# Attention scores kept as negatives with a running minimum, one reciprocal per group, and the output weights' casts queued behind the last exponential

## The chip, the cores and the metric

The kernel runs on one core of one Trainium2 chip. The metric is device time in microseconds (us) of one execution. The core has a matrix engine (TensorE, PE in the profile; PEld is its weight load), a vector engine (VectorE, DVE), an activation engine (ScalarE, ACT), GpSimd (POOL) and a queue that issues DMAs (SyncE, SP). Each engine works through its own queue strictly in order.

## The reference, cut to what matters

One decoder layer: half of the heads do dilated attention, half an mLSTM; the two are concatenated, projected with `w_out`, normalised, and followed by a mixture of 32 experts and a second normalisation. The change touches the attention heads alone, and the moment at which `w_out` is prepared.

```python
scores = einsum('bhrnqe,bhrnke->bhrnqk', qs, kb) * e ** -0.5
m = max(scores, axis=-1, keepdims=True)
p = exp(scores - m)
l = sum(p, axis=-1, keepdims=True)
o = einsum('bhrnqk,bhrnke->bhrnqe', p / l, vb)
...
y = concatenate([attn, hm], axis=-1) @ w_out
```

The kernel folds the three dilated branches into one softmax with an additive mask `am`: the logarithm of how often a key is counted, or -1e30 where it isn't seen.

## The kernel before, in words

The program is written with a planner: the Python order of the code is the priority, and the planner puts each engine's instructions into one fixed queue, in which something of lower priority goes first where the planner expects the higher one to be still waiting. `tc.high_priority` raises a block's priority. `tc.issue_after(ins)` queues every instruction of a block that runs on the engine of `ins` behind `ins` in that engine's queue; instructions of the block on other engines are not bound by it, except through their data.

The mixer takes the first 490 us, roughly, of the span. Its attention part loops over four pairs of heads, j = 0 to 3. A pair has 8 tiles of 128 queries for each of its 2 heads, in two groups: `scores(o, 0)` does query tiles 0 to 3, `scores(o, 1)` tiles 4 to 7 (lines 507 to 531). For query tile i the keys are 128*(i+1) long and are handled in pieces of up to 512 columns. Per piece two matmuls write the PSUM tile `s` (three buffers), and one fused DVE instruction (line 525, in the trace a CUSTOM_DVE with a short accumulator read behind it) adds the mask, writes the sum to SBUF as `p`, and keeps the running maximum in `mx`. Then, per tile and head, DVE negates the maximum (line 528), ACT computes the exponential in place with that bias and sums the row (line 529), and DVE takes the reciprocal of the sum (line 530). That is 64 tiles, 96 pieces.

`values(j, o, g, ...)` (lines 533 to 564) transposes the weights `p` on PE, copies them to SBUF (one head on ACT, the other on DVE), multiplies with the values (line 550), transposes the result back (line 559), and one DVE multiplication (line 561, `ao`) applies the reciprocals `rl` of the whole group. A DMA then writes `ao` to `mixd`.

Between these, `mlstm(c)` does chunk c of the mLSTM heads and `qk_proj(j + 1)` projects queries and keys of the next pair. The order is: `scores(o, 1)`, `mlstm(2j)`, `values(.., 0)`, then `qk_proj(j + 1)` or, for j = 3, `out_weights()`, then `mlstm(2j + 1)`, the next pair's `scores(o2, 0)`, and `values(.., 1)`.

`out_weights()` (lines 569 to 578) loads `w_out` in 8 parts of 128 rows into two buffers `woraw`, and splits each into a high part `woh` (ACT cast, line 111) and a low part `wol` (DVE subtraction, line 112, in the helper `split`). A buffer takes its next part only when the DVE subtraction of the part two before it is done; the DMA for that waits at the head of SP's queue. After the pairs, `project(t, n)` multiplies the mixed rows with `woh` and `wol` (line 683), and the rest of the kernel follows: routing, experts, final normalisation.

Of the kernel before, what the change touches and what calls it, by code (L numbers as in the profile page):

```python
# [14 lines left out]
AF = mybir.ActivationFunctionType  # L15
OP = mybir.AluOpType
# [14 lines left out]
NEG = -1.0e30  # L31
# [74 lines left out]
class Build:  # L106
# [29 lines left out]
    def mixer(self):  # L136
        nc, tc, I, C = self.nc, self.tc, self.I, self.C
# [176 lines left out]
        for g, dst in ((0, ip), (1, fp)):  # L314
            for hf in range(2):
                pt = ps.tile([4, 512], F32, name="m", bufs=1, padded_shape=[128, 512])
                for t in range(4):
# [15 lines left out]
                                     op0=OP.max, op1=OP.add)  # L333
# [31 lines left out]
        def qk_proj(j):  # L365
            hi, lo = [], []
            for g in range(2):
                raw, h, l = chunk([128, 4, 2, 128], "qk")
                for w in range(2):
                    nc.sync.dma_start(raw[:, :, w], I["w_in"][g * 512:(g + 1) * 512,  # L370
                                                            w * 512 + j * 128:w * 512 + (j + 1) * 128].rearrange(
                        "(k p) f -> p k f", p=128))
                self.split(h, l, raw)
                hi.append(h)
                lo.append(l)
            for w, dst, scale in ((0, qd, 0.125), (1, kd, 1.0)):
                for n in range(2):
                    ns = slice(n * 512, (n + 1) * 512)

                    def evict(a_):  # L380
                        h_ = self.pq.tile([128, 512], F32R, name="qh", tag="ev", bufs=4)
                        l_ = self.pq.tile([128, 512], F32R, name="ql", tag="ev", bufs=4)
                        nc.scalar.activation(h_, a_, AF.Copy, scale=scale)
                        nc.vector.scalar_tensor_tensor(l_, a_, scale, h_.bitcast(F32), op0=OP.mult, op1=OP.subtract)
                        for h in range(2):
                            nc.sync.dma_start(dst[2 * j + h, 0, :, ns], h_[64 * h:64 * h + 64].bitcast(F32))
                            nc.sync.dma_start(dst[2 * j + h, 1, :, ns], l_[64 * h:64 * h + 64].bitcast(F32))

                    w_tile(lambda k: (hi[k // 4][:, k % 4, w], lo[k // 4][:, k % 4, w]), n, evict)
# [3 lines left out]
        am = po.tile([128, S], F32, name="am")  # L393
# [113 lines left out]
        def scores(o, g):  # L507

            P = {}
            rl = pt_.tile([128, 4, 2], F32, name="rl", bufs=3)  # L510
            for i in range(4 * g, 4 * g + 4):
                nk = (i + 1) * 128
                off = S - nk
                for h in range(2):
                    q, kh, kl = o[h]
                    p = P[h, i] = pt_.tile([128, nk], F32, name=f"p{i}", bufs=2)
                    mx = pt_.tile([128, 4], F32, name="mx", bufs=4)
                    for n, a in enumerate(range(0, nk, 512)):
                        b = min(nk, a + 512)
                        s_ = ps.tile([128, 512], F32, name="s", bufs=N_S)  # L520
                        nc.tensor.matmul(s_[:, :b - a], q[:, i * 128:(i + 1) * 128], kh[:, a:b],
                                         start=True, stop=False)
                        nc.tensor.matmul(s_[:, :b - a], q[:, i * 128:(i + 1) * 128], kl[:, a:b],
                                         start=False, stop=True)
                        nc.vector.tensor_tensor_reduce(p[:, a:b], s_[:, :b - a], am[:, off + a:off + b], 1.0,
                                                       NEG if n == 0 else mx[:, 0:1], op0=OP.add, op1=OP.max,
                                                       accum_out=mx[:, n:n + 1])
                    nc.vector.tensor_scalar(mx[:, 2:3], mx[:, n:n + 1], -1.0, None, op0=OP.mult)
                    nc.scalar.activation(p, p, AF.Exp, bias=mx[:, 2:3], accum_out=mx[:, 3:4])
                    nc.vector.reciprocal(rl[:, i - 4 * g, h:h + 1], mx[:, 3:4])  # L530
            return P, rl

        def values(j, o, g, P, rl):

            oT = ps.tile([128, 512], F32, name="pv", bufs=1)
            nk = 4 * g + 4
            for k in range(nk):
                i0 = max(k, 4 * g)
                n = nk - i0
                pT, ev = [], []  # L540
                for h in range(2):
                    tp = ps.tile([128, 4, 128], F32, name="pT", bufs=N_PT)
                    for i in range(i0, nk):
                        nc.tensor.transpose(tp[:, i - i0], P[h, i][:, k * 128:(k + 1) * 128], ident)
                    t = pt_.tile([128, 4, 128], F32, name="pTs", bufs=N_PTS)
                    ev.append((nc.vector.tensor_copy if h else nc.scalar.copy)(t[:, :n], tp[:, :n]))
                    pT.append(t)

                with tc.high_priority(PAIR):
                    mms = [nc.tensor.matmul(oT[64 * h:64 * h + 64, (4 - n) * 128:], o["v"][:, k, 64 * h:64 * h + 64],  # L550
                                            pT[h][:, :n].rearrange("p a b -> p (a b)"), start=k == 0,
                                            stop=k == nk - 1, skip_group_check=True) for h in range(2)]
                self.after(mms[0], ev[1], mybir.DependencyClass.Sync)
                self.after(mms[1], mms[0])
            os_ = pt_.tile([128, 512], F32, name="os", tag="os", bufs=1)
            nc.scalar.copy(os_, oT)
            tp = ps.tile([128, 4, 128], F32, name="pT", bufs=N_PT)
            for i in range(4):
                nc.tensor.transpose(tp[:, i], os_[:, i * 128:(i + 1) * 128], ident)
            ao = pt_.tile([128, 4, 2, 64], F32, name="ao", tag="os", bufs=1)  # L560
            nc.vector.tensor_tensor(ao, tp.rearrange("p a (h e) -> p a h e", h=2),
                                    rl[:, :, :, None].to_broadcast([128, 4, 2, 64]), op=OP.mult)
            nc.sync.dma_start(mixd[g * 512:(g + 1) * 512, j * 128:(j + 1) * 128].rearrange("(a p) e -> p a e", p=128),
                              ao.rearrange("p a h e -> p a (h e)"))
# [4 lines left out]
        def out_weights():  # L569
            nonlocal pw, px, woh, wol  # L570
            pw = tc.alloc_tile_pool(name="pw", bufs=1, side="right", reuse_waits="tile")
            woh = pw.tile([128, 8, D], F32R, name="woh")
            wol = pw.tile([128, 8, D], F32R, name="wol")
            for k in range(8):
                raw = pw.tile([128, D], F32, name="woraw", bufs=2)
                nc.sync.dma_start(raw, I["w_out"][k * 128:(k + 1) * 128, :])
                self.split(woh[:, k, :], wol[:, k, :], raw)
            px = tc.alloc_tile_pool(name="px", bufs=1, side="right", reuse_waits="tile")
# [3 lines left out]
        def mixed(t):  # L582

            mx = px.tile([128, D], F32, name="mixt", bufs=2)
            nc.sync.dma_start(mx, mixd[t * 128:(t + 1) * 128, :])
            mh = px.tile([128, 8, 128], F32R, name="mh", bufs=2)
            ml = px.tile([128, 8, 128], F32R, name="ml", bufs=2)
            for g in range(2):
                tp = ps.tile([128, 4, 128], F32, name="s", bufs=N_S)
                for j in range(4):  # L590
                    nc.tensor.transpose(tp[:, j], mx[:, (4 * g + j) * 128:(4 * g + j + 1) * 128], ident)
                self.split(mh[:, 4 * g:4 * g + 4], ml[:, 4 * g:4 * g + 4], tp)
            mT[t] = mh, ml

        P0 = scores(o, 0)
        for j in range(4):
            P1 = scores(o, 1)
            mlstm(2 * j)
            values(j, o, 0, *P0)
            if j < 3:  # L600
                qk_proj(j + 1)
            else:
                self.pq.release()
                pa.release()
                out_weights()
                with tc.high_priority(PAIR):
                    mixed(0)
                split = self.lastv
            mlstm(2 * j + 1)
            if j < 3:  # L610
                o2 = operands(j + 1)
                P0 = scores(o2, 0)
            values(j, o, 1, *P1)
            if j < 3:
                o = o2
# [935 lines left out]
```

## Time and profile before

| what | us |
|---|---|
| median of 3 runs | 2060.92 (2059.4 to 2061.57) |
| the profiled execution | 2062.43 |
| span of the profiled execution | 2060.8 |
| PE busy | 1978.8 (96%) |
| DVE busy | 1531.8 (74%) |
| ACT busy | 1214.6 (59%) |

The span is the time from the first to the last instruction that the profiler recorded; the execution's own time lies 1.63 us above it. Busy times are sums over the whole span, and stages differ much. In the rows further down, a time in us from the span's start stands first, then a duration, the engine, the line of the kernel, the operation, output and input, and in brackets how long the engine sat idle before it and what ended that. "issue" there means that the wait was for nothing that the profile can name.

### The profile page before, as it was taken

The numbers are of one execution on the slowest core, as the hardware profiler recorded it, in microseconds if no ns is written. First come the engines' busy times: TensorE is split into PE (matmuls) and PEld (weight loads), VectorE is DVE, ScalarE is ACT, GpSimd is POOL, SyncE is SP. The second block draws the span as 40 slices with busy tenths as digits, with TensorE's granted clock in tenths as the row PEclk, the third lists the DMA queues.
The fourth block names the chain that finished last, engine by engine and source line by source line (L and its number), as shares of the span: only waits on it lengthen the run. The fifth ranks groups of instructions, "written<-read, shape, count | busy, mean of one in ns | idle before, by whom it ended". The sixth has DMA issues, their size and how long they took to land.

```text
span 2060.8 us, 33562 instructions
## 1 busy us (share of the span) xinstructions
PE 1978.8 (96%) x11575; PEld 1506.2 (73%) x11575; DVE 1531.8 (74%) x2351; ACT 1214.6 (59%) x1668; POOL 336.0 (16%) x162
## 2 busy tenths in 40 slices
PE   8999999989988999999999999999999999999992
PEld 7987676756766886677777777777777777777771
DVE  4263554576878686777979889798797887987886
ACT  4232544462226565666767767677676776766774
POOL 0000100100002030322303213033131330310100
PEclk9999999999998999999999999999999999999996
DMA  7327465556329678787988989989889898898985
GB/s 245 100 79 184 114 163 151 138 171 198 142 86 367 243 257 301 263 321 279 363 301 325 350 298 337 329 317 364 288 335 339 310 367 285 338 312 297 357 343 184
DMA packets 194782, 543.18 MB, mean 264 GB/s; under 512 B 23964, under 2 KB 60100, under 8 KB 194604
## 3 DMA queue, kind: packets, MB, share of 16 engines
q1 hardware_dynamic: 179760, 493.28, 66.4%
q0 software_dynamic: 13840, 44.57, 8.6%
q10 hardware_dynamic: 1008, 3.15, 0.4%
q8 instruction: 92, 1.51, 0.3%
q14 instruction: 82, 0.67, 0.1%
HBM read 486.10 MB, written 54.82 MB: 262 GB/s over the span
## 4 chain that ended last, share of the span: by engine, by line
PE 71%; DVE 3%; DMA 2%; ACT 1%; issue 1%; SPq 0%; DVEq 0%; POOLq 0%; ACTq 0%
PE mm L1162 53%; PE fold L1171 8%; PE tr L1125 3%; PE acc L683 2%; PE mm L1178 1%; PE s L683 1%; DMA acc<-ym,idx 1%; DMA raw<-in_w_gate 0%; PE tr L1047 0%; PE pv L550 0%; PE tr L1114 0%; DMA xt<-in_x 0%; ACT fs L1486 0%; PE pv L743 0%; DMA woraw<-in_w_out 0%
## 5 line engine op out<-in xcount | busy, mean ns | idle before, releaser
L112 DVE TENSOR_TENSOR wlo<-raw,whi 128x1024 fp32r<-128x1024 f32 x768 | 914.3, 1224 | 193.9 <-ACT whi L111 171.1
L111 ACT CAST whi<-raw 128x1024 fp32r<-128x1024 f32 x768 | 804.8, 1052 | 313.2 <-PE mm L1162 271.4
L1162 PE MATMUL mm<-whi,xh 128*128 128x512 f32 x1040 | 336.0, 404 | 0.0
L1162 PE MATMUL mm<-wlo,xh 128*128 128x512 f32 x1040 | 323.2, 392 | 0.0
L1162 PE MATMUL mm<-whi,xl 128*128 128x512 f32 x1040 | 321.8, 391 | 0.0
L1097 POOL DMA_INDIRECT acc<-ym,idx x35 | 69.6, 1988 | 985.1 <-DVE lst L1078 494.3
L1162 PEld LDWEIGHTS mm<-whi,xh 128*128 128x128 f32 x1040 | 186.2, 188 | 59.8 <-issue 24.0
L1162 PEld LDWEIGHTS mm<-whi,xl 128*128 128x128 f32 x1040 | 195.5, 188 | 43.0
L1162 PEld LDWEIGHTS mm<-wlo,xh 128*128 128x128 f32 x1040 | 195.6, 188 | 42.7
L1162 PE MATMUL mm<-whi,hh 128*128 128x512 f32 x528 | 169.6, 402 | 0.7 <-ACT hh L111 0.7
L1162 PE MATMUL mm<-whi,hl 128*128 128x512 f32 x528 | 166.2, 395 | 0.0
L1162 PE MATMUL mm<-wlo,hh 128*128 128x512 f32 x528 | 166.1, 395 | 0.0
L1092 POOL DMA_INDIRECT xm<-hs,idx x35 | 111.5, 3187 | 54.1 <-PE mm L1162 26.9
L1162 PEld LDWEIGHTS mm<-wlo,hh 128*128 128x128 f32 x528 | 99.4, 188 | 23.3
L1162 PEld LDWEIGHTS mm<-whi,hl 128*128 128x128 f32 x528 | 99.2, 188 | 23.2
L1162 PEld LDWEIGHTS mm<-whi,hh 128*128 128x128 f32 x528 | 96.1, 188 | 25.7 <-issue 4.9
L1092 POOL DMA_INDIRECT xf<-hs,idx x12 | 101.4, 8452 | 3.7 <-issue 3.7
L1171 PE MATMUL fold<-raw,xf 128*32 128x256 f32 x1536 | 87.9, 381 | 0.0
L238 PE MATMUL acc<-xh,whi 128*128 128x512 f32 x192 | 78.1, 407 | 0.1
L238 PE MATMUL acc<-xh,wlo 128*128 128x512 f32 x192 | 77.1, 402 | 0.0
L238 PE MATMUL acc<-xl,whi 128*128 128x512 f32 x192 | 76.8, 400 | 0.0
L1171 PEld LDWEIGHTS fold<-raw,xf 128*32 128x32 f32 x1536 | 47.3, 110 | 33.7 <-issue 4.7
(385 smaller groups left out, 2766.1 us busy)
## 6 DMA issues: line engine op xcount, KB each, us to landing
raw<-in_w_down SPq DMA_DIRECT2D x256, 512.0 KB
raw<-in_w_gate SPq DMA_DIRECT2D x252, 512.0 KB
raw<-in_w_up SPq DMA_DIRECT2D x252, 512.0 KB
wraw<-in_w_in SPq DMA_DIRECT2D x24, 256.0 KB
wraw<-in_w_in SPq DMA_DIRECT2D x8, 512.0 KB
aq<-qd SPq DMA_DIRECT2D x8, 512.0 KB
akh<-kd SPq DMA_DIRECT2D x16, 256.0 KB
akl<-kd SPq DMA_DIRECT2D x16, 256.0 KB
```

Of the source, the lines that this page charges most:

```text
L111: self.lasts = self.nc.scalar.copy(hi, src)
L112: self.lastv = self.nc.vector.tensor_tensor(lo, src, hi.bitcast(F32), op=OP.subtract)
L238: nc.tensor.matmul(a_, w, x[:, k, ns], start=(k == 0 and i == 0), stop=(k == 7 and i == 2))
L683: self.projected = nc.tensor.matmul(a_, a[:, k], b[:, k, ns], start=(k == 0 and i == 0), stop=(k == 7 and i == 2))
L1092: self.gathered = self.nc.gpsimd.indirect_dma_start(xg, None, self.rows(self.hs, kind), bass.IndirectOffsetOnAxis(ap=idx[:, u:u + 1], axis=0))
L1097: self.nc.gpsimd.indirect_dma_start(self.rows(self.acc, kind), bass.IndirectOffsetOnAxis(ap=idx[:, u:u + 1], axis=0), y, None, compute_op= ...
L1125: self.turned = nc.tensor.transpose(tp[:, j], x[:, (4 * g + j) * 128:(4 * g + j + 1) * 128], ident)
L1162: self.multiplied = nc.tensor.matmul(outs[n], a[:, kk], b[k][:, n * 512:(n + 1) * 512], start=first and kk == 0 and i == 0, stop=kk == 7 a ...
L1171: nc.tensor.matmul(out[m * g:m * g + m], x[:, kk % n, (kk // n) * m:(kk // n) * m + m], raw[:, g * w:(g + 1) * w], start=first and kk == 0 ...
L1178: self.nc.tensor.matmul(outs[n], self.ones[32 * n:32 * n + 3], brow[32 * n:32 * n + 3, w], start=first, stop=False)
```

## The change

Scores are written with the opposite sign: the fused DVE instruction now scales the masked sum by -1 and keeps a running minimum, which starts at +1e30. The minimum of the negatives is minus the maximum, so it serves as the bias of the exponential as it is, and the exponential takes a scale of -1. The sum of a row is written by ACT straight into its column of the group's tile `rl`, and `values` inverts that tile (128 x 8 values) with one reciprocal, in place, ahead of the multiplication. The block `out_weights()` is traced inside `issue_after` of the last exponential that has been traced, which for j = 3 is that of tile 7, head 1.

```diff
-    nc.vector.tensor_tensor_reduce(p[:, a:b], s_[:, :b - a], am[:, off + a:off + b], 1.0,
-                                   NEG if n == 0 else mx[:, 0:1], op0=OP.add, op1=OP.max,
+    nc.vector.tensor_tensor_reduce(p[:, a:b], s_[:, :b - a], am[:, off + a:off + b], -1.0,
+                                   -NEG if n == 0 else mx[:, 0:1], op0=OP.add, op1=OP.min,
                                    accum_out=mx[:, n:n + 1])
-nc.vector.tensor_scalar(mx[:, 2:3], mx[:, n:n + 1], -1.0, None, op0=OP.mult)
-nc.scalar.activation(p, p, AF.Exp, bias=mx[:, 2:3], accum_out=mx[:, 3:4])
-nc.vector.reciprocal(rl[:, i - 4 * g, h:h + 1], mx[:, 3:4])
+self.weighed = nc.scalar.activation(p, p, AF.Exp, bias=mx[:, n:n + 1], scale=-1.0,
+                                    accum_out=rl[:, i - 4 * g, h:h + 1])
...
+            nc.vector.reciprocal(rl, rl)
             nc.vector.tensor_tensor(ao, tp.rearrange("p a (h e) -> p a h e", h=2),
                                     rl[:, :, :, None].to_broadcast([128, 4, 2, 64]), op=OP.mult)
...
-                out_weights()
+                with tc.issue_after(self.weighed.ins):
+                    out_weights()
```

## Rows read from the trace of the kernel before

**Rows 1.** The page: busy time of PE, and the chain that ended last, by engine.
```profile
PE 1978.8 (96%) x11575; PEld 1506.2 (73%) x11575; DVE 1531.8 (74%) x2351; ACT 1214.6 (59%) x1668; POOL 336.0 (16%) x162
...
PE 71%; DVE 3%; DMA 2%; ACT 1%; issue 1%; SPq 0%; DVEq 0%; POOLq 0%; ACTq 0%
```

**Rows 2.** Timeline of PE where it sat idle, in the four stretches of scores.
```profile
222.55 0.33 PE L544 MATMUL pT<-cst,p 128*128 128x128 f32 x1 [0.54 <-ACT p L529]
...
233.49 0.68 PE L472 MATMUL m<-va,w 128*128 128x129 f32 x4 [2.23 <-issue]
...
310.17 0.49 PE L498 MATMUL m<-va,kw 128*128 128x129 f32 x2 [1.86 <-DVE mx L528]
...
375.06 0.46 PE L472 MATMUL m<-va,w 128*128 128x129 f32 x2 [0.65 <-DVE rl L530]
...
438.53 0.50 PE L521 MATMUL s<-akh,aq 128*128 128x512 f32 x1 [0.89 <-DVE mx L525]
443.06 0.77 PE L472 MATMUL m<-va,w 128*128 128x129 f32 x2 [2.46 <-issue]
```

**Rows 3.** Windows: stretch, length, busy PE, PEld, DVE, ACT, POOL, PE's clock, DMA.
```profile
233.50:237.00 3.50, 3.50 (x14) 1.93 (x15) 3.39 (x6) 2.33 (x6) 0.00 (x0) 0.64 0.08 11
237.00:240.00 3.00, 3.00 (x16) 2.04 (x16) 0.85 (x5) 2.12 (x8) 0.00 (x0) 0.85 1.10 301
...
312.00:316.00 4.00, 4.00 (x25) 2.39 (x25) 2.28 (x9) 2.79 (x13) 0.10 (x1) 1.00 0.53 130
...
443.00:446.00 3.00, 2.94 (x10) 1.66 (x10) 2.89 (x5) 2.13 (x5) 0.00 (x0) 0.50 0.00 0
```

**Rows 4.** Timeline of DVE: removed instructions, what starts next, the end of the last scores.
```profile
426.85 0.15 DVE L528 TENSOR_SCALAR mx<-mx 128x1 f32<-128x1 f32 x1
...
426.91 0.42 DVE L525 CUSTOM_DVE_ANT_0 p<-s,am 128x256 f32<-128x256 f32 x1
...
434.15 0.16 DVE L530 RECIPROCAL rl<-mx 128x1 f32<-128x1 f32 x1
434.23 0.47 DVE L525 CUSTOM_DVE_ANT_0 p<-s,am,mx 128x256 f32<-128x256 f32 x1
...
437.79 0.16 DVE L530 RECIPROCAL rl<-mx 128x1 f32<-128x1 f32 x1 [0.94 <-ACT p L529]
...
441.42 0.74 DVE L525 CUSTOM_DVE_ANT_0 p<-s,am,mx 128x512 f32<-128x512 f32 x1
...
442.28 0.68 DVE L462 TENSOR_TENSOR w<-m,w 128x512 f32<-128x512 f32 x1
```

**Rows 5.** Waits of DVE, 213 to 490 us: total us, times, longest.
```profile
DVE rl L530 <- ACT p L529: 4.7, 9, 0.9
```

**Rows 6.** Timeline of DVE: a chain of small instructions, each needing the one before.
```profile
449.07 0.15 DVE L478 SCALAR_TENSOR_TENSOR sm<-num 128x4 f32<-128x4 f32 x1
449.26 0.16 DVE L479 TENSOR_TENSOR sm<-sm,colt 128x4 f32<-128x4 f32 x1
```

**Rows 7.** Timeline of ACT: casts of `woh`, and the last exponential.
```profile
435.78 1.05 ACT L111 CAST woh<-woraw 128x1024 fp32r<-128x1024 f32 x1 [1.10 <-DMA woraw<-in_w_out]
...
438.58 1.04 ACT L111 CAST woh<-woraw 128x1024 fp32r<-128x1024 f32 x1
...
443.54 1.13 ACT L529 ACTIVATE p<-p,mx 128x1024 f32<-128x1024 f32 x1
...
451.25 1.03 ACT L111 CAST woh<-woraw 128x1024 fp32r<-128x1024 f32 x1
```

**Rows 8.** Timeline: DVE's second subtraction `wol`, SP's next loads of `woraw`.
```profile
444.94 1.20 DVE L112 TENSOR_TENSOR wol<-woraw,woh 128x1024 fp32r<-128x1024 f32 x1
445.02 1.54 SPq L576 DMA_DIRECT2D woraw<-in_w_out  x2
```

**Rows 9.** The chain that ended last, 200 to 660 us: start, us, what.
```profile
460.89 5.79 DMA woraw<-in_w_out
...
467.78 1.23 DVE wol L112
```

## The prediction

> **What bounds the kernel now.** I read the page first: PE is busy 96% of the span, and the chain that ended last is PE's for 71% [rows 1]. A change that shortens DVE and ACT work, as this one does, can bring time only where PE stands still for them. So the second view is PE's timeline in the mixer's attention part (213 to 490 us), idle times alone. There are four stretches of scores, one per pair of heads, and nearly every idle time of PE stands at the end of one: 0.54 and 2.23 us in the first, 1.86 in the second, 0.65 in the third, 0.89 and 2.46 in the last [rows 2]. Each ends in a DVE line of the scores, or in a product that needs a DVE result queued behind the scores: the two "issue" waits are for `w`, which DVE multiplies at line 462 after the last running maximum. DVE's in-order queue is the bound in these stretches; elsewhere between 240 and 424 us PE has hardly a gap.
>
> The third view is the clock. After the waits of 2.23 and 2.46 us PE was granted less than full clock: 0.64 for 3.5 us and 0.85 for 3 us after the first, 0.50 for 3 us after the other, which is the lower of its two levels, 1.2 GHz for 2.4; after the wait of 1.86 us it stayed at 1.00 [rows 2, 3]. Lost by that: 0.36 x 3.5 + 0.15 x 3 = 1.7 us, and 0.5 x 3 = 1.5 us. A gap that shrinks a little can so return more than its shrinking.
>
> The fourth view is the chain from 445 us on: the load of a part of `w_out` (5.79 us), its cast and its subtraction stand in it [rows 9], so what the change does to them decides how much of the last stretch's gain is kept.
>
> **The change part by part.** *Negations and reciprocals.* 64 of each go, one pair for each tile of scores, 0.15 and 0.16 us long [rows 4]. What counts is how soon the next instruction starts: 0.06 us after a negation (426.85 to 426.91), 0.08 after a reciprocal (434.15 to 434.23) [rows 4]. So 64 x 0.14 = 9.0 us of DVE's queue, 2.2 per pair. Besides, a reciprocal stands in DVE's queue until ACT has summed its row: 4.7 us of waits in 9 places, the longest 0.94 at 437.79 [rows 4, 5]. Those go too, unless the queue meets the same lateness at the next score. DVE thus loses 9.0 + 4.7 = 13.7 us at most, but PE can gain only what it idles.
>
> The Trainium skill (VectorE: DVE Perf Modes, The DRAIN you can't avoid) has it that the next vector instruction starts only when the pipe of the one before is empty. By that rule the removed pairs would cost their whole durations, 64 x 0.31 = 19.8 us, against 9.0; the starts in [rows 4] speak for the smaller, since the next one starts well inside the duration of the one before.
>
> *First stretch.* With DVE 2.2 us shorter, and some waits on ACT gone, PE's 0.54 goes, and the 2.23 shrinks. It can't vanish: behind PE's last score still come DVE's pass over it and the multiplication `w`, 0.74 and 0.68 us [rows 4], so about 1.4 us stay. That is 0.8 + 0.5, and up to 1.7 more if the clock holds, as it did behind the gap of 1.86 us (312 to 316 us) [rows 3]. I take 2.5 us; bounds 0.3 (only the last negation and reciprocals go, clock falls as before) and 4.5 (all of 0.54 + 2.23 + 1.7). *Second stretch:* 1.86 us of backlog against 2.2 removed: I take 1.2, bounds 0 and 1.9. *Third:* 0.4, bounds 0 and 0.65.
>
> *Casts of `woh` moved.* Two of the eight now stand among the last stretch's exponentials, 1.05 and 1.04 us, the first after 1.10 us in which ACT waited for the load [rows 7]; that is why DVE's reciprocal waited 0.94 us. With the bound they come behind the last exponential, which began at 443.54 and ended near 444.7. Without the two casts and the wait it would end 3.2 us earlier if ACT were the only bound; DVE's last score moves by about 2.2 + 0.94 = 3.1 as well. So the last exponential ends near 441.5, and the two casts follow to 443.6, DVE's subtractions to about 444.8. Today the second subtraction runs from 444.94 to 446.14, and SP's loads for the third and fourth part start at 445.02 [rows 8], held at the head of SP's queue behind the first subtraction. So the chain of loads starts about 1.3 us earlier, not 3. The loads themselves and the DVE subtractions are not bound by the new order; SP issues the first two loads as before. Queued behind the third load on SP are loads of the mLSTM's chunk 7, which move with it.
>
> *Last stretch.* PE's 0.89 goes, the 2.46 shrinks to about 1.6, and the clock may hold (1.5): up to 3.2 us, with all of the idle 4.85. What is late next is the chain of loads, cast and subtraction, up to which PE has other work in its queue. So I take 2.0, between 1.3 (the chain alone) and 3.2. Bounds: 4.85 above; below zero, minus 1.5, if the two casts slip behind a shorter piece of ACT's work each (a larger slip is a rival, below).
>
> *The new reciprocal.* 8 instead of 64, one ahead of each `ao`. The multiplication needs its result at once. In a chain of dependent small instructions the next starts 0.19 us after (449.07 to 449.26) [rows 6]. PE covers it in seven groups; in the last, where `ao` ends the mixer, it costs 0 (done early, its sums are there long before) to 0.2. I take 0.1. *The exponential* waits for one DVE instruction less; scale -1 and a column of `rl` as the sum's place I cost at nothing, like the minimum in place of the maximum: the trace shows neither, the nearest rows are the same instructions; to either side 0.02 us each on ACT, 64 of them, lies within the bounds above.
>
> Sum: 2.5 + 1.2 + 0.4 + 2.0 - 0.1 = 6.0 us. What follows the mixer is chained to its end (PE holds its queue through projection, routing and experts), so it moves along. The profiled execution took 2062.43, its span 2060.8, 1.63 us outside; it becomes 2056.4. It lies 1.5 above the median of the runs, 2060.92, which becomes 2054.9. By the bounds: 0.3 + 0 + 0 - 1.5 - 0.2 = -1.4, and 4.5 + 1.9 + 0.65 + 4.85 = 11.9; so 2062.3 to 2049.0.
>
> **The rivals.** *PE's own order is the bound.* PE gets its scores in a fixed queue with other work between; a faster DVE may only wait for PE instead, and the gap at the end of a stretch stays, as last score, pass and `w` follow each other. For: in none of the stretches but the last does PE wait long for a score. Against: the 1.86 us is plain backlog. Gain then 0.5 + 0.5 + 0.2 + 0.5 = 1.7: 2059.2, no change.
>
> *The casts come late.* The bound says "not before the last exponential", not "right behind it". In the queue the mLSTM's and the values' ACT work has the higher priority, and the third cast stands only at 451.25 today [rows 7]. Should the first two slip into such gaps, the second subtraction ends near 453.5 instead of 446.1, and each refill of the two buffers waits for it: 7.4 us on the chain of [rows 9]. Of that goes what the first three stretches bring, 4.1 us by the forecast, 1.2 by the rival before: plus 3.3 to plus 6.2, in the middle 2065.6, slower. It decides against the change from the point at which the second subtraction ends later than 446.1 + 4.1 = 450.2. Against: behind the last exponential ACT has to wait for PE's and DVE's results, and a cast fits there.
>
> *DVE leaves the path altogether.* All idle times and both losses of clock go: 11.9 us, 2049.0. The skill's rule quoted above (VectorE: DVE Perf Modes) leads here. It needs the planner to put `w` ahead of the last scores. I give it little.
>
> Beside these the planner draws up all queues anew; that may cost or bring some 3 us anywhere, which I fold into the chances.
>
> **How the numbers follow.** Forecast 2054.9: 0.44. DVE off the path, 2049.0: 0.11. PE's order, 2059.2: 0.28. Late casts, 2065.6: 0.17. A measurement of this kernel can tell 0.2%, 4.1 us, from no change: faster is below 2056.8, slower above 2065.0. The forecast's own range, 2051.5 to 2058.5, lies partly above 2056.8, which takes some 0.05 from it; of PE's order 0.04 falls below by a lucky order; of the late casts 0.03 stay within. So faster 0.54, same 0.32, slower 0.14. The range 2049.0 to 2063.5 takes in the bounds and the planner's play, and leaves out most of the late casts and a little below.
>
> **What would show it.** Right: PE's gaps near 233 and 443 us under 1.9 us and the clock at 1.00 behind them; the gap near 310 under 1; no cast of `woh` before the last exponential, the first two within 3 us behind it, and `ao` of the last group 5 to 6 us earlier than before. Wrong: gaps as before with DVE idle in front of its scores (PE's order), or the second subtraction after 450 us (late casts).

## The result, and the profile after

The changed kernel takes 2051.31 us in the median of 5 runs (2050.48 to 2052.00), the kernel before 2061.57 beside it. The ratio is 0.995, with a 95% interval of 0.9939 to 0.996: 10.3 us, or 0.5%, faster. Predicted were 2054.9 us and a gain of 6.0; the range, 2049.0 to 2063.5, held the time. The time lies 0.2 below the span of 2051.5 to 2058.5 that the prediction gave its forecast alone, 3.6 below the forecast and 2.3 above the point of the rival that takes DVE off the path (2049.0). The profiled execution took 2051.31 us, its span 2049.6, against 2062.43 and 2060.8.

First the page of the changed kernel: busy time of the engines, and the chain that ended last, by engine.

```profile
PE 1971.4 (96%) x11575; PEld 1503.0 (73%) x11575; DVE 1518.6 (74%) x2231; ACT 1211.4 (59%) x1668; POOL 337.3 (16%) x162
...
PE 88%; DVE 5%; DMA 3%; ACT 2%; issue 1%; SPq 1%; POOL 0%; DVEq 0%; POOLq 0%; ACTq 0%
```

DVE has 120 instructions fewer (64 + 64 - 8) and is busy 13.2 us less [rows 1]. Lines 529 to 560 of before now have numbers lower by one: the exponential is line 528, and the new reciprocal is line 560.

Next PE's timeline with its idle times, in the same part as [rows 2]. These are the first stretch's only gap by DVE, a gap in the third, and the two longest of the last.

```profile
221.53 0.50 PE L521 MATMUL s<-akh,aq 128*128 128x512 f32 x1 [0.27 <-DVE mx L525]
...
361.09 0.49 PE L474 MATMUL m<-Ct,wi 128*128 128x129 f32 x2 [0.77 <-POOL wi L466]
...
428.19 0.49 PE L474 MATMUL m<-Ct,wi 128*128 128x129 f32 x2 [2.29 <-POOL wi L466]
...
449.82 0.94 PE L461 MATMUL m<-qT,kT 128*128 128x128 f32 x6 [1.48 <-DVE kw L454]
```

The waits of 0.54 and 2.23 us in the first stretch and of 1.86 in the second are not smaller but gone. In the last, 0.89 and 2.46 are gone too, but 2.29 stands at 428, for something else: `wi`, which POOL makes from a loaded tile. The waits for DVE's `kw` have grown there: 0.89 us at 417.57, where the kernel before waits 0.45 at 426.44, and 1.48 at 449.82, where it has no wait above 0.2.

The windows, columns as in [rows 3], say what the clock did. The first three windows answer to rows of before; the fourth is the wait for `wi`, the fifth what follows it.

```profile
233.50:237.00 3.50, 3.50 (x20) 2.32 (x19) 2.26 (x9) 3.50 (x10) 0.00 (x0) 1.00 0.42 120
237.00:240.00 3.00, 3.00 (x21) 1.91 (x21) 1.10 (x4) 2.55 (x11) 0.10 (x1) 1.00 0.30 90
312.00:316.00 4.00, 4.00 (x24) 3.35 (x23) 1.20 (x3) 1.67 (x3) 0.00 (x0) 1.00 0.77 175
425.90:428.20 2.30, 0.01 (x1) 0.02 (x1) 1.27 (x6) 1.54 (x4) 1.27 (x1) 1.00 0.96 356
428.20:432.00 3.80, 3.80 (x12) 1.98 (x13) 0.49 (x2) 0.17 (x2) 0.30 (x1) 0.56 0.34 102
```

The clock holds at 1.00 behind the first stretch, where it was 0.64 and 0.85. Behind the new wait it is 0.56, close to the lower level, 1.2 of 2.4 GHz.

**Where the gain is.** I set the start of each group's `ao` (DVE, line 561) against before, counted from the first query projection of the mLSTM (PE, line 442: 214.82 us before, 214.53 after). The `ao` of groups 2, 3, 6 and 7 start at 288.82, 318.58, 424.85 and 453.97 before and at 282.44, 310.57, 416.23 and 444.23 after; the first `z` (the projection's sum) starts at 491.89 and 482.61. Gained up to there: 6.1, 7.7, 8.3, 9.4 and 9.0 us. So 8.3 of the mixer's 9.0 are there by the sixth `ao`, the end of the first three stretches. Some 0.7 of them is work of PE that has moved behind that point: from there to `z` PE is busy 58.08 us, before 57.43. What follows `z` brings 1.9 more. PE's next wait, for `z`, is 0.90 us instead of 2.62, and the clock behind it stays at 1.00, where before it was 0.50 for 3.4 us; against that stands a new wait of 1.03 us at 498.16, for DVE's `ml`.

**Why the first stretch's gap went wholly.** DVE's timeline, its last scores of that stretch and `w`; in the kernel before:

```profile
231.84 0.75 DVE L525 CUSTOM_DVE_ANT_0 p<-s,am,mx 128x512 f32<-128x512 f32 x1
...
232.71 0.68 DVE L462 TENSOR_TENSOR w<-m,w 128x512 f32<-128x512 f32 x1
```

In the changed kernel:

```profile
228.43 0.68 DVE L462 TENSOR_TENSOR w<-m,w 128x512 f32<-128x512 f32 x1
...
231.56 0.75 DVE L525 CUSTOM_DVE_ANT_0 p<-s,am,mx 128x512 f32<-128x512 f32 x1
...
233.94 0.74 DVE L525 CUSTOM_DVE_ANT_0 p<-s,am,mx 128x512 f32<-128x512 f32 x1
```

The planner has put `w` 5.5 us ahead of the last score; before, it came right behind it. PE's next product no longer waits for the end of the scores. DVE now waits for PE's scores oftener; its waits, 213 to 490 us (total, times, longest), in which the wait of the reciprocal for ACT, 4.7 us in 9 places [rows 5], has all but gone:

```profile
DVE p L525 <- PE s L523: 55.8, 18, 40.6
...
DVE rl L560 <- ACT p L528: 0.2, 1, 0.2
```

(In the kernel before the first of these was 46.1 us in 7 places, the same 40.6 among them.)

**The casts.** ACT's timeline of the changed kernel: the last exponential, and the first casts of `woh` [rows 7].

```profile
438.91 1.15 ACT L528 ACTIVATE p<-p,mx 128x1024 f32<-128x1024 f32 x1
...
440.98 1.04 ACT L111 CAST woh<-woraw 128x1024 fp32r<-128x1024 f32 x1
...
443.45 1.04 ACT L111 CAST woh<-woraw 128x1024 fp32r<-128x1024 f32 x1
...
448.42 1.05 ACT L111 CAST woh<-woraw 128x1024 fp32r<-128x1024 f32 x1 [0.79 <-DMA woraw<-in_w_out]
```

The last exponential begins 4.6 us earlier, the casts follow 0.9 and 3.4 us behind its end, and DVE's second subtraction `wol` runs from 444.84 to 446.06, where before it ended at 446.14 [rows 8].

**The wait that is now last in the fourth stretch.** Pieces of the chain that ended last:

```profile
416.23 0.70 DVE ao L561
416.95 0.38 SPq L563
417.42 0.56 SPq L433
418.07 0.59 SPq L435
418.75 7.97 DMA wi<-wid
426.86 1.28 POOL wi L466
428.19 0.49 PE m L474 x2
```

SP's queue holds the loads of the next mLSTM chunk behind the store of `ao`; the load of `wi` is the third behind it and takes 8 us to land. This wait isn't new in kind. The kernel before has it in its second stretch, in a row of PE's timeline that I passed over:

```profile
300.04 0.49 PE L474 MATMUL m<-Ct,wi 128*128 128x129 f32 x2 [1.49 <-POOL wi L466]
```

With the changed queues it is gone there, and stands at 361 and 428 instead. Its length is not set by the queues alone: the kernel before with the bound added, whose queues are the same up to 424 us, waits 0.45 us at that place.

### The profile page after: what moved, and what is told of

It is laid out like the page before. It is cut to its first block, busy times and chain, and to the rows that moved or that the text cites. A ratio compares the mean times of both kernels' runs of the same rounds, so it can differ in the third digit from the quotient of the medians.

```text
span 2049.6 us, 33420 instructions
## 1 busy us (share of the span) xinstructions
PE 1971.4 (96%) x11575; PEld 1503.0 (73%) x11575; DVE 1518.6 (74%) x2231; ACT 1211.4 (59%) x1668; POOL 337.3 (16%) x162
## 4 chain that ended last, share of the span: by engine, by line
PE 88%; DVE 5%; DMA 3%; ACT 2%; issue 1%; SPq 1%; POOL 0%; DVEq 0%; POOLq 0%; ACTq 0%
PE mm L1163 53%; PE fold L1172 8%; PE acc L238 5%; PE acc L228 4%; PE tr L1126 3%; PE v L197 2%; PE acc L684 2%; PE pv L549 2%; PE mm L1179 1%; PE pT L543 1%; PE s L684 1%; DMA wi<-wid 1%; PE s L521 1%; DMA acc<-ym,idx 1%; DMA raw<-in_w_gate 1%
## 5 line engine op out<-in xcount | busy, mean ns | idle before, releaser
L525 DVE CUSTOM_DVE_ANT_0 p<-s,am 128x512 f32<-128x512 f32 (+3 forms) x64 | 36.0, 588 | 52.2 <-PE s L523 51.2
```

## The experiments

None of them leaves out work, and each was timed beside the kernel before. The letters in the expectations are theories; each text says what its letter expects. Two measures stand together: the ratio of the times, with its interval, and the length of the mixer in the profile, from the first line 442 product to the first `z`, set against 277.1 us before. Four pairs of kernels differ by the bound alone, and the two of a pair have the same queues up to 427 us or later. Counted so, their sixth `ao` lie 1.0 us apart (with both parts of the change), 1.3 (with none), 2.0 (sign) and 0.5 (reciprocals). So a difference of up to 2 us in the mixer can be the spread of executions. Single executions of one kernel lie up to 11 us apart (before: 2056.09 to 2066.99 in one set). From `z` to the end the profiles take between 1565.8 and 1570.4 us. So a difference of 2 or 3 us between medians that the mixer doesn't show can't be placed.

| kernel | ratio to before | gain in time, us | gain in the mixer, us |
|---|---|---|---|
| changed | 0.9950 (0.9939 to 0.9960) | 10.3 | 9.0 |
| without the bound | 0.9972 (0.9962 to 0.9982) | 5.8 | 4.8 |
| bound alone | 1.0006 (0.9996 to 1.0016) | -1.2 | -1.6 |
| sign alone | 0.9993 (0.9983 to 1.0002) | 1.4 | 5.1 |
| reciprocals alone | 0.9973 (0.9960 to 0.9986) | 5.6 | 5.5 |
| sign and bound | 0.9965 (0.9951 to 0.9979) | 7.2 | 3.2 |
| reciprocals and bound | 0.9964 (0.9953 to 0.9974) | 7.4 | 7.6 |
| changed, 128 small DVE instructions put in | 0.9980 (0.9968 to 0.9993) | 4.1 | 1.3 |
| before, heads swapped | 1.0008 (0.9994 to 1.0023) | -1.6 | -0.8 |
| changed, heads swapped | 0.9950 (0.9933 to 0.9968) | 10.3 | 9.3 |
| changed, `wi` loaded first | 0.9949 (0.9931 to 0.9967) | 10.5 | 8.8 |
| changed, two loads from POOL | 0.9985 (0.9974 to 0.9997) | 3.1 | 4.4 |
| changed, store from ACT | 0.9963 (0.9949 to 0.9977) | 7.6 | 10.2 |

(Gain in time: one minus the ratio, times 2061 us.)

**The changed kernel without the bound.**

```diff
-                with tc.issue_after(self.weighed.ins):
-                    out_weights()
+                out_weights()
```

> The changed kernel without the bound on out_weights: negatives, minimum and one reciprocal per group stay. Theory A (the time came out of DVE's queue in the scores, the bound on the casts adds little, since by the changed kernel's trace the group's end moved only 0.4 to 1 us more in the last stretch than before it): 2051 to 2053.5 us, the last ao near 474 to 476. Rival B (the bound is what makes the last stretch): 2055 us or more, with casts of woh among the exponentials again and ACT waiting for a load there.

Measured were 2055.85 us, a gain of 5.8: theory A (2051 to 2053.5) missed, B (2055 or more) held. The bound holds 4.5 of the 10.3 us. Up to the sixth `ao`, where the queues of the two are the same, nothing is lost (9.4 us gained, against 8.3). All of it goes in the last stretch. ACT's timeline of this kernel:

```profile
428.35 1.04 ACT L111 CAST woh<-woraw 128x1024 fp32r<-128x1024 f32 x1 [1.76 <-DMA woraw<-in_w_out]
430.21 1.04 ACT L111 CAST woh<-woraw 128x1024 fp32r<-128x1024 f32 x1 [0.82 <-DMA woraw<-in_w_out]
...
440.95 1.05 ACT L111 CAST woh<-woraw 128x1024 fp32r<-128x1024 f32 x1
441.90 1.15 ACT L528 ACTIVATE p<-p,mx 128x1024 f32<-128x1024 f32 x1
...
448.37 1.04 ACT L111 CAST woh<-woraw 128x1024 fp32r<-128x1024 f32 x1 [3.63 <-DMA woraw<-in_w_out]
...
449.72 0.56 ACT L555 COPY os<-pv 128x512 f32<-128x512 f32 x1
```

Three casts stand ahead of the last exponential, which begins 1.8 us later than in the changed kernel, counted from the line 442 product; the fourth waits 3.63 us for its load, with the copy `os` queued behind it, and PE waits for `os`:

```profile
450.34 1.11 PE L558 MATMUL pT<-cst,os 128*128 128x128 f32 x4 [2.92 <-ACT os L555]
```

The clock had fallen before that wait and stays down beyond it (columns as in [rows 3]; in the changed kernel it is 1.00 from 445 to 455 us):

```profile
445.00:455.10 10.10, 7.18 (x35) 6.56 (x33) 4.89 (x14) 5.81 (x14) 1.38 (x3) 0.50 0.62 197
```

Behind the wait for `wi`, here 2.44 us, it is 0.50 from 428.4 to 434.6 us too, in the changed kernel 0.56 for 3.8 us. From 445.0 to 455.1 PE is busy 7.18 us; at full clock that work would take about half of it (an estimate), so much of what is lost is clock. In this kernel a cast that waits for its load holds up ACT's queue, and that is what the bound keeps out; how much the clock would have lost without it is not shown.

**The bound alone, on the kernel before.**

```diff
-                    nc.scalar.activation(p, p, AF.Exp, bias=mx[:, 2:3], accum_out=mx[:, 3:4])
+                    self.weighed = nc.scalar.activation(p, p, AF.Exp, bias=mx[:, 2:3], accum_out=mx[:, 3:4])
...
-                out_weights()
+                with tc.issue_after(self.weighed.ins):
+                    out_weights()
```

> The kernel before with the bound alone: casts of woh behind the last exponential, negations and reciprocals as before. Theory A: DVE's 0.94 us wait and part of PE's gaps in the last stretch go, nothing before 424 us: 1 to 2 us less than before, 2059.5 to 2060.5. Rival B: 4 us less or more. Rival C (late casts cost, hidden in the changed kernel by DVE's gain): 1 to 4 us more than before.

Measured were 2062.56 us: it brings nothing, and A (2059.5 to 2060.5) missed. C (1 to 4 us more) is nearer: 1.2 more by the ratio, whose interval takes in no change, and 1.6 in the mixer, of which 1.3 stand at the sixth `ao`, before the bound can act. The gap of 2.46 us stays, at 2.24, since DVE's queue is as long as before, and the casts start at 447.72, so the chain of loads ends later: the last subtraction starts at 476.58, before at 470.33, 5.5 us later counted as above. By itself the bound is worth nothing.

**One part at a time.** Sign and minimum alone (lines 525 and 526 as in the change) keep the 64 reciprocals; the grouped reciprocal alone keeps the 64 negations. Neither has the bound.

```diff
+                    nc.scalar.activation(p, p, AF.Exp, bias=mx[:, n:n + 1], scale=-1.0, accum_out=mx[:, 3:4])
```

> The kernel before with the sign and the minimum changed and the 64 negations gone; 64 reciprocals stay, each behind its exponential in DVE's queue. Theory A, by queue time alone: 64 x 0.06 us = 3.8 of the 9.0 us, a third to a half of the gain in the first two stretches: 2056 to 2059. Rival D (what counts is DVE's waiting for ACT at the reciprocals): under 1.5 us less than before. Rival E (the planner's new order is the cause, not the length): anything, without relation to the parts.

```diff
+                    nc.scalar.activation(p, p, AF.Exp, bias=mx[:, 2:3], accum_out=rl[:, i - 4 * g, h:h + 1])
...
+            nc.vector.reciprocal(rl, rl)
```

> The kernel before with ACT writing the sums into rl and one reciprocal per group; 64 negations stay. Theory A, by queue time alone: 64 x 0.08 us and the waits on ACT: 4 to 6 us less than before, 2055.5 to 2057.5. Rival D (the waits are what counts): nearly the whole gain, 2052 to 2054. Rival E (order): the gains of this and of the sign alone don't add up to the one of both without the bound.

Measured were 2059.94 and 2055.43 us. For the sign A (2056 to 2059) missed by 0.9, and the rival D (under 1.5 us of gain) holds by the ratio's 1.4; for the reciprocals A (2055.5 to 2057.5) missed by 0.07, with the 4 to 6 us of gain that it named, and D (2052 to 2054) missed. The traces speak for A in both: up to the sixth `ao` sign alone gains 6.6 us and the reciprocals alone 5.8, each well over half of the 9.4 that both bring without the bound: they don't add up. Rival E, the planner's new order, expected that too. Both parts shorten the same queue and PE has only so much idle time to give, which would do the same; these two runs don't tell the one from the other. In the last stretch all three fall back to about 5 us at `z` (5.1, 5.5 and 4.8). In the time the sign alone shows 1.4 us where its mixer shows 5.1. Behind `z` its profiled execution loses 1.2 of that; most of the rest is that this execution, 2058.14 us, is the second fastest of 10 and lies 1.8 below their median.

**One part and the bound.** The two kernels above, with the bound as in the change.

> The kernel before with sign and minimum changed and the bound added; 64 reciprocals stay. In the trace of the sign alone the groups up to 424 us ended 6.6 us earlier, of which 1.3 to 4 were lost again among the casts. Theory I (the bound keeps in the last stretch what a shorter DVE queue brings before it, and brings nothing by itself): 2054 to 2056. Rival J (the bound helps only where both kinds of small instructions are gone): as the sign alone, 2058.5 to 2060.

> The kernel before with one reciprocal per group and the bound added; 64 negations stay. In the trace of the reciprocals alone the groups up to 424 us ended 5.8 us earlier and the last one 5.0. Theory I: little is left for the bound, 2054 to 2056, about 1 us less than the reciprocals alone. Rival J: as the reciprocals alone, 2055 to 2056.5; more than 2 us of gain from the bound would speak for a third thing.

Measured were 2055.12 and 2054.62 us, both within the 2054 to 2056 of theory I, that the bound keeps what a shorter queue brings. But the traces bear out only half of it. With the reciprocals the bound brings the mixer 2.1 us more and the time 1.8. With the sign the time shrinks by 5.8 by the ratios, while the mixer is 2.0 us longer, which fits J. Those 2.0 us are not the bound's: they are there at the sixth `ao`, with a wait of 2.15 us for `wi` at 296.84, where the sign alone, with the same queues, waits 0.06 at 293.99. Where the 5.8 us lie the profiles can't say: the profiled execution of the sign alone is among the fastest of its set and the one with the bound the slowest of its 7, and these two are 0.4 us apart (2058.14 and 2057.74).

The bound can act only behind the sixth `ao`. From there to `z` it brings the mixer 5.2 us with both parts of the change, 2.6 with the reciprocals, nothing with the sign and -0.4 on the kernel before. So it pays in the two kernels with the grouped reciprocal and in neither of the two others; why is open.

**The queue's length by itself.** The changed kernel, with two small multiplications per tile into a tile that nobody reads. They take the place of negation and reciprocal in DVE's queue, but wait for no ACT sum, and the exponential doesn't wait for them.

```diff
+                    du = pt_.tile([128, 2], F32, name="du", bufs=4)
+                    nc.vector.tensor_scalar(du[:, 0:1], mx[:, n:n + 1], -1.0, None, op0=OP.mult)
+                    nc.vector.tensor_scalar(du[:, 1:2], mx[:, n:n + 1], -1.0, None, op0=OP.mult)
```

> The changed kernel with two small DVE instructions per tile of scores put back, 128 in all, each of the size of the removed ones, which write a scratch tile that nobody reads and wait for nothing of ACT's. Theory A1 (length of DVE's queue is what brought the time): 128 x 0.06 us = 7.7 us back on DVE, most of the gain is lost, 2055 to 2058. Theory A2 (what brought it is that DVE's queue no longer stands for ACT's sums): under 2 us lost, 2051 to 2053.

Measured were 2056.97 us, within the 2055 to 2058 expected if the queue's length is the cause (A1), outside the 2051 to 2053 of A2. PE's gaps of before come back. Its timeline, and the windows behind the first gap:

```profile
232.76 1.65 PE L461 MATMUL m<-qT,kT 128*128 128x128 f32 x6 [2.23 <-DVE kw L454]
...
310.15 0.49 PE L498 MATMUL m<-va,kw 128*128 128x129 f32 x2 [1.71 <-DVE Ct L500]
...
376.91 1.16 PE L461 MATMUL m<-qT,kT 128*128 128x128 f32 x8 [1.73 <-DVE kw L454]
...
444.10 0.77 PE L472 MATMUL m<-va,w 128*128 128x129 f32 x2 [2.34 <-issue]
```

```profile
232.80:236.00 3.20, 3.20 (x10) 1.61 (x10) 2.83 (x4) 1.15 (x3) 0.00 (x0) 0.50 0.09 10
236.00:240.00 4.00, 4.00 (x17) 3.35 (x16) 1.31 (x3) 0.37 (x1) 0.00 (x0) 0.61 0.91 254
```

At the sixth `ao` this kernel is 2.2 us behind the one before: 10.6 us behind the changed one, all of the gain of the first three stretches and more. So that gain hangs on the length of DVE's queue. The reciprocals' waits for ACT have no share that can be seen there: this kernel has none of them, and is no faster up to there than the kernel before, which has them all. The length works at least in part through the order that the planner draws from it: here `kw` (232.02) and `w` (237.08) stand behind the last score of the first stretch, in the changed kernel `w` stands ahead of it. No run shortens the queue and keeps its order, so the two aren't separated.

Behind the sixth `ao` this kernel gains 3.5 us on the one before, where the bound alone, with a queue of about the same length, loses 0.4. Something other than the length brings that; DVE no longer waits for ACT's sums and the exponentials no longer wait for a negation, but which of these it is no run shows. So 4.1 of the 10.3 us stay in the time.

**The queues drawn anew, with no work changed.** Head 1 ahead of head 0 in the scores, in the kernel before and in the changed one.

```diff
-                for h in range(2):
+                for h in (1, 0):
```

> The kernel before with the two heads of a pair traced in the other order within scores: the same instructions, the same dependences, another order of the queues. It measures how much a new drawing of the queues alone moves the time. Theory A (length and waits are the cause): within 2 us of before. Rival E (the order is the cause): 4 us or more to either side.

> The changed kernel with the two heads of a pair traced in the other order within scores; bound as before to the exponential traced last, now that of head 0. Theory A: within 2 us of the changed kernel. Rival E: 4 us or more to either side.

Measured were 2062.91 and 2051.91 us; neither moves from its kernel, as theory A had it. Within the mixer the order does move something: the swapped kernel before stands 4.0 us ahead of its kernel at the sixth `ao`, and loses 4.8 from there to `z`. The 10.6 us that the put-in instructions take away up to the sixth `ao` are well beyond that, and by this one other drawing the 10.3 us of the time are not a lucky one.

**Three tries at the wait for `wi`.** Its load traced at the head of `mlstm(c)`; the loads of `va` and `wi` issued by POOL; the store of `ao` issued by ACT.

```diff
+            if c:
+                wi = pm.tile([128, 4, 128], F32, name="wi", bufs=1)
+                nc.sync.dma_start(wi, wid[None, :, cs].to_broadcast([128, 4, 128]))
...
-                wi = pm.tile([128, 4, 128], F32, name="wi", bufs=1)
-                nc.sync.dma_start(wi, wid[None, :, cs].to_broadcast([128, 4, 128]))
```

> The changed kernel with the mLSTM's load of wi traced at the head of mlstm instead of behind its scores. In the changed kernel's trace PE stands 2.29 us at 428.19 for GpSimd's wi, which waited for its load: SP issued it at 418.75, behind the store of ao, and it landed 8 us later; PE's clock fell behind that gap. Theory F (this load is what is late next where DVE was): the gap goes, 2 to 4 us less than the changed kernel, 2047.5 to 2049.5. Rival G (the chain of the parts of w_out ends the mixer anyway): within 1 us of the changed kernel.

Measured were 2051.24 us; F (2047.5 to 2049.5) missed, G (no change) held. The gap passes to the next load in the queue, `va`, which now comes behind `wi`; PE's timeline:

```profile
425.59 0.77 PE L473 MATMUL m<-va,w 128*128 128x129 f32 x2 [2.40 <-DMA va<-vmd]
```

```diff
-            nc.sync.dma_start(va[:, :, 0:128], vmd[cs, :].rearrange("t (h f) -> t h f", h=4))
+            nc.gpsimd.dma_start(va[:, :, 0:128], vmd[cs, :].rearrange("t (h f) -> t h f", h=4))
...
-                nc.sync.dma_start(wi, wid[None, :, cs].to_broadcast([128, 4, 128]))
+                nc.gpsimd.dma_start(wi, wid[None, :, cs].to_broadcast([128, 4, 128]))
```

> The changed kernel with the mLSTM's loads of va and wi issued from GpSimd's queue instead of SyncE's. With the load of wi alone moved ahead, the gap of PE near 427 us passed on to va, which SP issued behind the store of ao too. Theory F2 (SP's order, a store that waits for ao at its head, is what is late next): the gap near 427 goes, with the loss of clock behind it 2 to 4 us less than the changed kernel, 2047 to 2049.5. Rival G (the chain of the parts of w_out ends the mixer): within 1 us of the changed kernel, the parts' last subtraction as before at 467. Rival H (transfers from GpSimd's queue start later): the gap grows, 2052 or more.

Measured were 2058.27 us, where F2 had 2047 to 2049.5. H (2052 or more, since the gap grows) has the time but not the cause: the gap at 428 is gone, and yet the kernel is slower than the changed one by some 7 us, 4.6 of them in the mixer. Other waits have come; PE's timeline:

```profile
305.93 0.49 PE L498 MATMUL m<-va,kw 128*128 128x129 f32 x2 [1.36 <-DVE Ct L500]
...
415.52 0.33 PE L521 MATMUL s<-akh,aq 128*128 128x128 f32 x1 [1.85 <-DMA akh<-kd]
...
442.16 0.49 PE L498 MATMUL m<-va,kw 128*128 128x129 f32 x2 [1.96 <-DVE Ct L500]
```

```diff
-            nc.sync.dma_start(mixd[g * 512:(g + 1) * 512, j * 128:(j + 1) * 128].rearrange("(a p) e -> p a e", p=128),
+            nc.scalar.dma_start(mixd[g * 512:(g + 1) * 512, j * 128:(j + 1) * 128].rearrange("(a p) e -> p a e", p=128),
```

> The changed kernel with the store of ao issued from ScalarE's queue instead of SyncE's, so that the mLSTM's loads no longer stand behind a store that waits for ao. Theory F3 (SP's order makes the gap near 427, and the gap costs): the loads of va, og and wi start 2 us earlier, the gap shrinks below 1 us, 1 to 3 us less than the changed kernel, 2048.5 to 2050.5. Rival G (the gap is covered by what ends the mixer anyway, the chain of the parts of w_out): within 1 us of the changed kernel, the last subtraction of the parts near 467 as before. Rival K (SP is then held by the load of v, which waits for the last product of the pair before): the loads start no earlier, the gap stays.

Measured were 2052.09 us; F3 (2048.5 to 2050.5) missed, G (within 1 us of the changed kernel) held. SP issues the load of `wi` at 415.23 instead of 418.75, but PE is earlier too, the load again takes 8.0 us, and PE still waits 2.46 us at 424.71. The mixer is 1.2 us shorter than the changed kernel's, which is within the spread, and the gain by the ratio is 2.7 smaller, with intervals that overlap. None of the three beats the change.

## Why the prediction was right, and where its sizes were off

**The bound of the stretches: right.** DVE's queue held PE in them, and a shorter queue, with the order that the planner drew from it, gave back the gaps of the first two stretches and the clock of the first. The same number of small instructions put in again takes all of it away up to the sixth `ao`. One reading was loose: the wait of 0.54 us ended in ACT's exponential and not in a DVE line [rows 2].

**First stretch: 2.5 forecast, 4.2 in idle time and clock.** From 213 to 240 us PE is busy 25.72 us, before 22.89, and its mean clock is 1.00, before 0.94: 2.8 us, and 0.06 x 22.89 = 1.4. That is nearly the upper bound, 4.5. The step that failed is "it can't vanish: behind PE's last score still come DVE's pass over it and the multiplication `w`". It took the order of DVE's queue as fixed, and the planner put `w` ahead. The rival "DVE leaves the path altogether" had named the condition, `w` ahead of the last scores, and I gave it little; in this stretch it came true. (At the second `ao` the gain is 6.1. The 1.9 beyond these 4.2 is work of PE that now comes a group later: between the first and the second `ao` PE is busy 41.11 us, before 43.41, and between the second and the third 27.88, before 26.18.) The 1.4 of clock need not have been there to win: the kernel before with its heads swapped has the same wait of 2.23 us and kept its clock, as the last section shows.

**Second stretch: 1.2 forecast, 3.3.** Between the second and the third `ao` PE idles 0.25 us, before 3.58. My upper bound was the 1.86 at 310.17 [rows 2]. The rest is the 1.49 at 300.04 for `wi`, which I left out of the sum since it ended in no line of the scores. Part of that is luck: with the bound alone and the same queues the wait for `wi` was 0.45. The third `ao` shows 7.7 us, against 4.2 + 3.3 = 7.5. **Third: 0.4 forecast, nothing in idle time.** The 0.65 for DVE is gone, but 0.77 for `wi` stands at 361.09 in its place: from the third to the sixth `ao` PE idles 1.92 us, before 1.75. What the sixth `ao` gains over the third is work moved, as said above.

**Last stretch: 2.0 forecast, 1.3 in idle time, none in clock.** From the sixth `ao` to `z` PE idles 8.30 us, before 9.61. DVE's gaps of 0.89 and 2.46 went as foreseen, but the wait for `wi`, 2.29 us with a clock of 0.56 for 3.8 us behind it, took their place, and the waits for `kw` grew. The mean clock from the sixth to the seventh `ao` is 0.94, as before. The prediction asked what is late next and answered with the chain of `woraw` alone. The second step that failed is the chain's start: the second subtraction was to end at 444.8 and ended at 446.06, because mLSTM work on ACT (`sq`, `os`) and the `ao` on DVE stood between. The first two casts came within 3.4 us of the last exponential, where I had said 3. The late casts of the rival (slower, 450.2 as its point) didn't come.

**The bound's worth: not seen.** I counted its gain inside the last stretch, as two casts taken from among the exponentials. On the shorter queue it is worth 4.5 us, since the casts would else have moved further forward, to 428 us, where their loads have not landed. The prediction took the casts' places from the trace of before, and a shorter queue moves them.

**The new reciprocal: 0.1 forecast, nothing seen.** It takes 0.20 us and is issued well ahead of `ao`: the seventh at 440.52, its `ao` at 444.23. Once it waits for ACT, 0.2 us. **Scale and sum's place: nothing, as said.** The exponentials' median is 762 ns, before 768.

**What follows moves along: nearly.** It gains 1.9 us more than the mixer in the profiles; the wait for `z` was 1.7 shorter and the clock held behind it, and 1.03 us of a new wait go against that.

The last `ao` starts 9.0 us earlier (482.76 to 473.75), where I had said 5 to 6.

The sum so: 0.3 ahead of the mixer, 4.2 + 3.3 - 0.2 + 1.3 = 8.6 in it, 1.9 behind, 10.8 of the 11.2 between the two spans; the other 0.4 is neither idle time nor clock. The sum of the forecast was 6.0, low in the first two stretches by 3.8 and high in the other two by 1.3, so its errors partly cancel.

**The rule of the skill.** By the Trainium skill (VectorE: DVE Perf Modes, The DRAIN you can't avoid) 128 small instructions would hold the queue for 19.8 us, an estimate with the durations of the removed ones. By their starts it is 9.0. Of the kernel that puts 128 in, DVE's timeline:

```profile
231.77 0.15 DVE L529 TENSOR_SCALAR du<-mx 128x1 f32<-128x1 f32 x1
231.84 0.14 DVE L530 TENSOR_SCALAR du<-mx 128x1 f32<-128x1 f32 x1
231.90 0.14 DVE L529 TENSOR_SCALAR du<-mx 128x1 f32<-128x1 f32 x1
231.96 0.14 DVE L530 TENSOR_SCALAR du<-mx 128x1 f32<-128x1 f32 x1
232.02 0.68 DVE L454 TENSOR_TENSOR kw<-m,colt 128x512 f32<-128x512 f32 x1
```

One starts every 0.06 to 0.07 us, inside the 0.14 of the one before, and 128 x 0.065 = 8.3 us. The rows decide for the smaller figure. The same section of the Trainium skill adds that a next instruction that is not held starts earlier, and points to a later one (Two Vector instructions with no wait between them); with that these rows agree.

**Open** are how much of the first stretches is the queue's length and how much the order drawn from it, where in the time the 5.8 us of the bound on the sign lie, what gives the kernel with the put-in instructions its 3.5 us in the last stretch, and what in the planner's new order made the loads from POOL a loss.

## What to carry to other kernels

Where a planner draws the queues, don't keep the old order when you cost a shorter queue: ask which product the planner can now pull ahead, since a gap that looks like a fixed tail can vanish with its loss of clock. List every idle time of the engine that bounds, also those that the change doesn't seem to touch, and look which of them stands next in each stretch. Work that waits for a load should be bound behind the work that others wait for, and such a bound has to be judged together with the change that makes it matter: alone it brought nothing, here 4.5 us. Before a wait is booked to a change, look whether another execution with the same queues has it too.

## What the hardware showed that I had not expected

The clock behind a wait is not told by the wait's length alone. In the kernel before a wait of 1.86 us at 310 left it at 1.00 [rows 2, 3]; with the small instructions put in, a wait of 1.71 us at the same place is followed by 0.60 for 3.4 us. PE had been busy 2.32 of the 4 us from 306 to 310 in the one and 2.44 in the other, so that doesn't tell them apart either. Nor does the order of the work: the kernel before with the bound alone has the same queues up to there and nearly the same wait, 1.84 us, and its clock fell to 0.63. The other way round, the kernel before with its heads swapped has the wait of 2.23 us in the first stretch that cost the kernel before its clock [rows 2, 3], and kept its own. A row of PE's timeline and a window behind it, first with the bound alone, then with the heads swapped:

```profile
310.55 0.49 PE L498 MATMUL m<-va,kw 128*128 128x129 f32 x2 [1.84 <-DVE mx L528]
310.50:314.00 3.50, 3.21 (x10) 1.42 (x11) 1.85 (x8) 3.23 (x11) 0.00 (x0) 0.63 0.56 118
```

```profile
233.95 0.68 PE L472 MATMUL m<-va,w 128*128 128x129 f32 x4 [2.23 <-issue]
234.00:237.50 3.50, 3.50 (x21) 2.27 (x22) 3.39 (x7) 2.89 (x9) 0.00 (x0) 1.00 0.12 20
```

What decides it is open; a gain of clock behind a short wait can so come or go from one execution to the next.

The load of `wi` (128 x 512 f32, 256 KB) doesn't take a fixed time either. It took 8.0 us to land at 418.75 in the changed kernel and at 415.23 with the store issued by ACT. With the sign alone POOL could start on it 6.0 us after its issue at 286.60, and with the bound added, the queues being the same up to there, 8.4 us after its issue at 287.08.
